# Six rotating PSUM banks outside the mixers, and a first feed forward that opens with four half-token results

## The chip, the cores and the metric

The kernel runs on one core of a Trainium2 chip. The time is that of the device, in microseconds (us), for one execution of the whole program. Before the change it is 1611.54 us, the median of 3 runs (1611.43 to 1612.52). The profile is one more execution, of 1611.52 us, whose span (first to last recorded instruction) is 1609.6 us.

## The reference

Two transformer blocks on 512 tokens of width 1024, in fp32. What matters here are the two feed forwards and the norms ahead of them:

```python
def first_block(x, c, ...):
    ...                                             # adaptive scales, sparse attention, retention, merge
    x = x + gate1 * jnp.dot(merged, w_out)
    h2 = _rmsnorm(x, norm2_w) * (1.0 + scale2) + shift2
    ffn = jnp.dot(jax.nn.silu(jnp.dot(h2, w_ffn_gate)) * jnp.dot(h2, w_ffn_up), w_ffn_down)
    x = x + gate2 * ffn
    return _rmsnorm(x, final_norm_w)

def second_block(x, ...):
    ...                                             # block-sparse attention, gated linear attention
    h = h + jnp.concatenate([o_nsa, o_gla], axis=-1) @ w_out
    u = causal_dwconv(rms_norm(h, ffn_norm) @ w_up, conv_w, conv_b)
    gate, up = jnp.split(u, 2, axis=-1)
    return h + (jax.nn.silu(gate) * up) @ w_down
```

The hidden width is 2816, that is 22 tiles of 128.

## The kernel before

Activations lie transposed: 128 features on the partitions, 512 tokens along a row. An fp32 product is made of three products (`mm3`, L298): activations and weights are each split into a high part and a rest, and high by high (L300), rest by high (L301) and high by rest (L302) are summed in one PSUM bank. "hH" and "hL" are the two parts of the activations, "wh" and "wl" those of a weight unit. A unit is one tile of 128 outputs by 8 tiles of 128 inputs, 512 KB. `load` (L280) fetches it into a staging tile "st" (3 buffers) by a DMA of SP's queue, ACT casts it to "wh" (L294) and DVE subtracts the rest "wl" (L295), each in two halves; "wh" and "wl" have 3 buffers each, so a fourth unit waits until the first is used up.

`projA` makes one tile of outputs for all 512 tokens: 24 products into one bank. `projM` makes several tiles at once, first for tokens 0 to 255 and then for tokens 256 to 511.

PSUM has eight banks. `ps` (L304) hands them out by tag: "mm" 3 banks for projections, "tr" 2 for transposes and small products, "pv" 1, and 2 for the attention scores ("at", or one tile of two banks; `scores` changes between the two forms). A projection takes an "mm" bank and must wait until the result that lay there three projections earlier has been read.

The end of block 1: `w_out` (L753) is done for tokens 0 to 255 and then for 256 to 511. After each half `norm2` (L629) does the norm: the sum of squares "acc" (L421, L422) goes through `tok_sum`, a product with a column of ones that puts the sums on the token's partition (L397); POOL takes the power -0.5 (L388, L389); `bcast` spreads the result over all partitions by products of ones and a diagonal "dg" (L409, L410); ACT copies that to "rbc" (L411); then for eight tiles DVE multiplies (L643), ACT or DVE scales and shifts (L648, L646), ACT casts "hH" (L380) and DVE or POOL makes "hL" (L381). These are the small products of the norm. While the second half of the tokens goes through this, `ffn1` (L997) has `projM` make the first half of three results: gate 0, up 0 and gate 1. From then on it uses `projA`: 22 pairs of gate and up, then 8 tiles of the down product.

The second feed forward `ffn2` (L1499) has no norm ahead of its products: they run on the raw sums, and each result is multiplied by "rbc" when DVE reads it from PSUM (L1517). So the banks of its first results come free only when the norm's broadcast is there.

The order of each engine's stream is set at build time, by a scheduler that takes instructions in the order in which the code issues them and moves them ahead where it finds a gap; `issue_after(x)` tells it to place an instruction only behind x. At run time each engine takes its stream strictly in order.

Of the kernel before, what the change touches and what calls it, by code (L numbers as in the profile page):

```python
# [8 lines left out]
F32 = mybir.dt.float32  # L9
F32R = mybir.dt.float32r  # L10
# [6 lines left out]
P = 128  # L17
# [149 lines left out]
class Builder:  # L167
    def __init__(self, nc, tc, ins, out, cdec, dbg=None):
        self.nc, self.tc, self.ins, self.out, self.cdec, self.dbg = nc, tc, ins, out, cdec, dbg or {}
        self.tasks, self.pend, self.ready = [], [], []  # L170
        self.order = self.plan()
        self.pools = {}
        self.every = 4
        self.deep = (4, 5)

# [98 lines left out]
    def ahead(self, n):  # L274

        while len(self.ready) < n and self.order:
            key = self.order.pop(0)
            self.ready.append((key, self.load(self.source(key))))

    def load(self, src, pool=None, eng=None):  # L280

        nc = self.nc
        a, b = src.shape[1], src.shape[2]
        n = a * b
        st = self.wp.tile([P, 1168], F32, name="st", tag="st", bufs=3)
        nc.sync.dma_start(st[:, 0:n], src.rearrange("p a b -> p (a b)"))
        if pool is None:
            hi = self.wp.tile([P, 1168], F32R, name="wh", tag="wh", bufs=3)
            lo = self.wp.tile([P, 1168], F32R, name="wl", tag="wl", bufs=3)
        else:  # L290
            hi, lo = [pool.tile([P, 1168], F32R, name=x) for x in ("wh0", "wl0")]
        cut = (a // 2) * b
        for x0, x1 in ((0, cut), (cut, n)):
            nc.scalar.copy(hi[:, x0:x1], st[:, x0:x1])  # L294
            (eng or nc.vector).tensor_tensor(lo[:, x0:x1], st[:, x0:x1], hi[:, x0:x1].bitcast(F32), op=ALU.subtract)  # L295
        return (hi[:, 0:n].rearrange("p (a b) -> p a b", b=b), lo[:, 0:n].rearrange("p (a b) -> p a b", b=b))
# [6 lines left out]

    def ps(self, tag):  # L304
        if tag == "at":
            return self.pa.tile([P, 512], F32, name="ps_at", tag="at", bufs=2) if self.apart else self.ps2()[0]
        return self.pp.tile([P, 512], F32, name="ps_" + tag, tag=tag, bufs={"mm": 3, "tr": 2, "pv": 1}[tag])
# [37 lines left out]

    def projM(self, keys, act):

        aH, aL = act
        U = [self.unit(x) for x in keys]
        ps = [self.ps("mm") for i in range(len(keys))]  # L350
        for hs in range(2):
            ts = slice(hs * 256, hs * 256 + 256)
            for n, ((H, L), p) in enumerate(zip(U, ps)):
                for k in range(8):
                    self.mm3(p[:, ts], H[:, k, :], L[:, k, :], aH[:, k, ts], aL[:, k, ts], k == 0, k == 7)
                if hs:
                    self.ahead(n + 1)
# [33 lines left out]
    def tok_sum(self, acc, name):  # L391
# [4 lines left out]
        for t in range(n):  # L396
            nc.tensor.matmul(ps[:, t:t + 1], acc[:, t * P:(t + 1) * P], self.ones[:, 0:1], start=True, stop=True)  # L397
        o = self.small.tile([P, NT], F32, name=name)
# [3 lines left out]
    def bcast(self, col, out):  # L402
# [4 lines left out]
        for t in range(n):  # L407
            dg = self.wk.tile([P, P], F32, name="dg", tag="dg", bufs=3)
            nc.vector.tensor_scalar(dg, self.c("ident"), col[:, t:t + 1], None, op0=ALU.mult)  # L409
            nc.tensor.matmul(ps[:, t * P:(t + 1) * P], self.ones, dg, start=True, stop=True)  # L410
        nc.scalar.copy(out, ps[:, 0:n * P])  # L411
# [122 lines left out]
    def build(self):  # L534
        nc, tc = self.nc, self.tc
        with tc.tile_pool(name="psum", bufs=1, space=PSUM) as self.pp, tc.tile_pool(name="dram", bufs=1, space=DRAM) as dp:
# [11 lines left out]
            self.ffn1()  # L548
            self.scores(True)
            self.block2_mix()  # L550
            self.close("scores")
            self.ffn2()
            self.close("x", "wk", "h", "w", "small", "cst")
# [75 lines left out]
    def norm2(self, acc, ts):  # L629

        nc = self.nc
        ss = self.tok_sum(acc, "ss2")
        rs = self.small.tile([P, NT], F32, name="rs2")
        n = acc.shape[1]
        self.rsq(rs[:, 0:n // P], ss[:, 0:n // P], 1.0 / D)
        rbc = self.wk.tile([P, S], F32, name="rbc", tag="rbc", bufs=2)
        self.bcast(rs[:, 0:n // P], rbc[:, 0:n])
        for j in range(8):
            if ts.start == 0:
# [12 lines left out]
    def block1_mix(self):  # L652
# [56 lines left out]
        with tc.manual_schedule(engines={mybir.EngineType.PE}):  # L709
# [4 lines left out]
            self.every = 4  # L714
        self.close("b1r", "b1a", "wa")
        self.dump("att", qaT)
        self.dump("y", y)
# [279 lines left out]
    def ffn1(self):  # L997
        nc, ins = self.nc, self.ins
        f1 = self.open("f1")
        first = self.projM([("wfg", 0), ("wfu", 0), ("wfg", 1)], self.act)  # L1000
        mods = self.add(self.mod_rest(40, 48), 0.25)
        mH = f1.tile([P, KF, S], F32R, name="fH")
        mL = f1.tile([P, KF, S], F32R, name="fL")
        for m in range(KF):
            pg = self.projA([("wfg", m)], self.act) if m > 1 else first[2 * m]
            s = self.wk.tile([P, S], F32, name="fs", tag="w2k", bufs=4)
            nc.scalar.activation(s, pg, AF.Silu)
            pu = self.projA([("wfu", m)], self.act) if m else first[1]
            nc.vector.tensor_tensor(s, pu, s, op=ALU.mult)
# [3 lines left out]
        nc.vector.tensor_tensor(self.fwan, self.v("final"), self.v("attn2"), op=ALU.mult)  # L1013
        acc1, acc2 = [f1.tile([P, S], F32, name=f"acc{i}") for i in range(2)]
        for m in range(8):
# [16 lines left out]
    def block2_mix(self):  # L1032
        nc, tc, ins = self.nc, self.tc, self.ins
        b2 = self.open("b2", "right")
        gmask = b2.tile([P, P], I32, name="gmask")
# [99 lines left out]
        self.finish()  # L1135
        self.close("gla", "wa", "bk")
        self.xT = self.open("x").tile([P, KD, S], F32, name="xT")
        po = self.open("o")
# [416 lines left out]
```

## Time and profile before

| what | value |
|---|---|
| time, median of 3 runs | 1611.54 us |
| the profiled execution | 1611.52 us |
| its span | 1609.6 us |
| PE busy | 1581.5 us, 98% |
| DVE busy | 952.1 us, 59% |
| ACT busy | 685.6 us, 43% |
| PE on the chain that ended last | 96% |

The PE (TensorE) is nearly always busy, so the table alone names no place to look at. The windows of 50 us do: in most of them PE is busy for all 50 us at a granted clock of 1.00, and in a few something is missing. A clock below 1.00 is a mean over the window of the two levels that TensorE has, 1.2 GHz and 2.4 GHz: 0.97 over 50 us means some 3 us at half clock.

### The profile page before, as it was taken

How to read it: one execution, taken by the hardware profiler on the slowest of the kernel's cores; microseconds unless marked ns; L12 is line 12 of the kernel's file. 1: busy time of each engine (PE TensorE's matmuls, PEld its weight loads, DVE VectorE, ACT ScalarE, POOL GpSimd, SP SyncE). 2: the span in 40 equal slices, each digit the busy share in tenths (PEclk: the TensorE clock that was granted, in tenths of full speed). 3: DMA queues.
4: the chain of work that ended last, by engine and by line, in shares of the span. 5: the costliest groups of instructions: out<-in, count | busy, mean ns of one | idle time of the engine just before them, and what ended most of it. 6: DMA issues, size and time to landing. Idle time of an engine off the chain costs nothing.

```text
span 1609.6 us, 23843 instructions
## 1 busy us (share of the span) xinstructions
PE 1581.5 (98%) x9093; PEld 1342.8 (83%) x9093; DVE 952.1 (59%) x2209; ACT 685.6 (43%) x1458; POOL 136.8 (8%) x290
## 2 busy tenths in 40 slices
PE   7999999999999999999999999999989999999999
PEld 5999888888888978888888899988768788888887
DVE  4468865477786764444333455676765777777221
ACT  4554765643223542232233334665643444444221
POOL 0130000121110110000000015100100000000000
PEclk9999999999999999999999999999999999999999
DMA  9223221236653533333333353121022222223331
GB/s 375 67 66 100 67 79 53 68 104 214 183 182 124 175 116 121 117 118 92 91 106 110 122 159 108 53 79 40 15 79 92 85 99 92 92 97 93 110 108 51
DMA packets 49440, 173.12 MB, mean 108 GB/s; under 512 B 6048, under 2 KB 6736, under 8 KB 48304
## 3 DMA queue, kind: packets, MB, share of 16 engines
q1 hardware_dynamic: 43376, 152.22, 29.5%
q0 software_dynamic: 5952, 19.40, 3.7%
q8 instruction: 71, 1.16, 0.3%
q14 instruction: 41, 0.34, 0.1%
HBM read 166.88 MB, written 4.19 MB: 106 GB/s over the span
## 4 chain that ended last, share of the span: by engine, by line
PE 96%; ACT 1%; DVE 1%; DMA 1%; issue 0%; POOL 0%; SPq 0%; POOLq 0%; ACTq 0%
PE ps_mm L300 28%; PE ps_mm L301 27%; PE ps_mm L302 27%; PE ps_tr L452 3%; PE ps_pv L506 2%; PE ps_at L1280 1%; PE ps_at L1229 1%; PE ps_at L891 1%; PE ps_at L833 1%; PE ps_at L966 0%; PE ps_at L1300 0%; DMA xs<-in_x_dram 0%; PE ps_pv L581 0%; PE ps_tr L410 0%; DMA xT<-xd 0%
## 5 line engine op out<-in xcount | busy, mean ns | idle before, releaser
L294 ACT CAST wh<-st 128x512 fp32r<-128x512 f32 (+3 forms) x508 | 283.7, 607 | 543.3 <-issue 265.9
L295 DVE TENSOR_TENSOR wl<-st,wh 128x512 fp32r<-128x512 f32 (+3 forms) x508 | 324.8, 670 | 172.1 <-ACT wh L294 170.2
L300 PE MATMUL ps_mm<-hH,wh 128*128 128x512 f32 (+1 forms) x1000 | 393.9, 394 | 4.4 <-DVE us L1517 2.2
L301 PE MATMUL ps_mm<-hL,wh 128*128 128x512 f32 (+1 forms) x1000 | 390.6, 391 | 0.3 <-DVE hL L381 0.3
L302 PE MATMUL ps_mm<-hH,wl 128*128 128x512 f32 (+1 forms) x1000 | 389.2, 390 | 0.0
L300 PEld LDWEIGHTS ps_mm<-hH,wh 128*128 128x128 f32 x1000 | 189.4, 189 | 45.1 <-DVE us L1517 2.4
L302 PEld LDWEIGHTS ps_mm<-hH,wl 128*128 128x128 f32 x1000 | 189.0, 189 | 41.0
L301 PEld LDWEIGHTS ps_mm<-hL,wh 128*128 128x128 f32 x1000 | 189.2, 189 | 38.6 <-DVE hL L381 0.5
L300 PE MATMUL ps_mm<-wh,hH 128*128 128x256 f32 (+2 forms) x672 | 192.8, 290 | 0.4 <-ACT hH L593 0.4
L301 PE MATMUL ps_mm<-wl,hH 128*128 128x256 f32 (+2 forms) x672 | 191.6, 287 | 0.0
L302 PE MATMUL ps_mm<-wh,hL 128*128 128x256 f32 (+2 forms) x672 | 189.1, 286 | 2.3 <-DVE hL L595 2.3
L300 PE MATMUL ps_mm<-fH,wh 128*128 128x512 f32 x352 | 138.8, 394 | 0.0
L301 PE MATMUL ps_mm<-fL,wh 128*128 128x512 f32 x352 | 138.7, 394 | 0.0
L302 PE MATMUL ps_mm<-fH,wl 128*128 128x512 f32 x352 | 138.5, 393 | 0.0
L300 PEld LDWEIGHTS ps_mm<-wh,hH 128*128 128x128 f32 x672 | 126.0, 188 | 5.2 <-issue 3.6
L302 PEld LDWEIGHTS ps_mm<-wh,hL 128*128 128x128 f32 x672 | 125.7, 189 | 3.4 <-DVE hL L595 2.8
L301 PEld LDWEIGHTS ps_mm<-wl,hH 128*128 128x128 f32 x672 | 126.4, 189 | 2.2 <-issue 1.4
L623 DVE SCALAR_TENSOR_TENSOR ma<-ms,silu_c,ma 128x128 f32<-128x128 f32 x224 | 77.3, 349 | 5.1
L300 PEld LDWEIGHTS ps_mm<-fH,wh 128*128 128x128 f32 x352 | 66.3, 188 | 15.4
L302 PEld LDWEIGHTS ps_mm<-fH,wl 128*128 128x128 f32 x352 | 66.1, 188 | 15.5
L301 PEld LDWEIGHTS ps_mm<-fL,wh 128*128 128x128 f32 x352 | 66.2, 188 | 15.1
L478 ACT ACTIVATE pm<-lt,mn 128x128 f32<-128x128 f32 (+3 forms) x96 | 53.8, 561 | 22.5 <-DVE mn L475 21.5
(376 smaller groups left out, 2195.2 us busy)
## 6 DMA issues: line engine op xcount, KB each, us to landing
st<-in_wup_dram SPq DMA_DIRECT2D x44, 512.0 KB, 3.3
ms<-in_wada_dram POOLq DMA_DIRECT2D x64, 256.0 KB, 3.4
st<-in_wo_dram SPq DMA_DIRECT2D x24, 512.0 KB, 3.5
st<-in_wfg_dram SPq DMA_DIRECT2D x22, 512.0 KB, 3.5
st<-in_wfu_dram SPq DMA_DIRECT2D x22, 512.0 KB, 3.5
wa<-in_wada_dram SPq DMA_DIRECT2D x8, 1024.0 KB, 11.6
st<-in_wret_dram SPq DMA_DIRECT2D x16, 512.0 KB, 3.6
st<-in_wfd_dram SPq DMA_DIRECT2D x16, 448.0 KB, 3.4
```

Source lines behind the costliest of these rows:

```text
L294: nc.scalar.copy(hi[:, x0:x1], st[:, x0:x1])
L295: (eng or nc.vector).tensor_tensor(lo[:, x0:x1], st[:, x0:x1], hi[:, x0:x1].bitcast(F32), op=ALU.subtract)
L300: mm(ps, lh, rh, start=start, stop=False)
L301: mm(ps, lh, rl, start=False, stop=False)
L302: mm(ps, ll, rh, start=False, stop=stop)
L452: return self.nc.tensor.transpose(out, src, self.c("ident", 0, n)[0:n])
L478: nc.scalar.activation(pm[:, 0:n], lt[:, 0:n], AF.Exp, bias=mn, scale=-1.0, accum_out=sm[:, a:a + 1])
L506: run(lambda: nc.tensor.matmul(pv()[a * 64:a * 64 + 64, j_, :], vtok(cc, 2 * j_ + a), PT_[a][:, cc * P:(cc + 1) * P], start=a not in start ...
L623: nc.vector.scalar_tensor_tensor(acc, w[:, k, :], s, acc, op0=ALU.mult, op1=ALU.add)
L833: nc.tensor.matmul(ps[:, 0:n], qS[:, h, :], ikS[:, i, 0:n], start=(i == 0), stop=(i == 1))
L891: run(lambda: nc.tensor.matmul(sc[:, 0:n], qaT[rows, h // 2, ts], kaT[rows, h // 2, 0:n], start=True, stop=True))
L1229: nc.tensor.matmul(ps[m][:, 0:64], w[:, i, m * P:(m + 1) * P], tb[:, ii, :, :].rearrange("p g n -> p (g n)"), start=(ii == 0), stop=(ii == ...
```

## The change

`ps` gets a counter "wide". While it is not None, every request for an "mm" bank is answered in turn with a bank of tag mm, at, mm, at, mm, pv: six banks that rotate. It is set to 0 at the end of block 1's mixers, taken away for those of block 2, and set again behind them. For this `scores(True)`, which brings the form with two single "at" banks, moves to the end of block 1's mixers, and the pool is closed only after `ffn2`.

`ffn1` opens with four half-token results instead of three: (up, 1) joins them. Its weights get a place of their own ("wh0", "wl0", in the pool f1), since the three usual buffers are taken. To make room, the two accumulators of `ffn1` move to the two "rbc" buffers of the pool wk. And two of the norm's small products get fixed places among the first half-token products: none from the 17th `mm3` on stands ahead of the sums (L397 before), none from the 27th on ahead of the broadcast (L410 before).

```diff
     def ahead(self, n):
-            self.ready.append((key, self.load(self.source(key))))
+            self.ready.append((key, self.load(self.source(key), pool=self.home.get(key))))
     def load(self, src, pool=None, eng=None):
-            hi, lo = [pool.tile([P, 1168], F32R, name=x) for x in ("wh0", "wl0")]
+            hi, lo = [pool.tile([P, n], F32R, name=x) for x in ("wh0", "wl0")]
     def ps(self, tag):
+        if tag == "mm" and self.wide is not None:
+            self.wide += 1
+            tag = ("mm", "at", "mm", "at", "mm", "pv")[self.wide % 6]
-    def projM(self, keys, act):
+    def projM(self, keys, act, between=()):
+        between = list(between)
+        count, behind = 0, None
...
                 for k in range(8):
-                    self.mm3(p[:, ts], H[:, k, :], L[:, k, :], aH[:, k, ts], aL[:, k, ts], k == 0, k == 7)
+                    if between and count == between[0][0]:
+                        behind = between.pop(0)[1]
+                    count += 1
+                    with self.tc.issue_after(behind) if behind is not None else contextlib.nullcontext():
+                        self.mm3(p[:, ts], H[:, k, :], L[:, k, :], aH[:, k, ts], aL[:, k, ts], k == 0, k == 7)
...
     def build(self):
             self.ffn1()
-            self.scores(True)
             self.block2_mix()
+            self.ffn2()
             self.close("scores")
-            self.ffn2()
     def norm2(self, acc, ts):
         ss = self.tok_sum(acc, "ss2")
+        sums = self.last
...
         self.bcast(rs[:, 0:n // P], rbc[:, 0:n])
+        self.marks = [sums, self.last]
     def block1_mix(self):
         self.close("b1r", "b1a", "wa")
+        self.scores(True)
+        self.wide = 0
     def ffn1(self):
-        first = self.projM([("wfg", 0), ("wfu", 0), ("wfg", 1)], self.act)
+        self.home["wfu", 1] = f1
+        first = self.projM([("wfg", 0), ("wfu", 0), ("wfg", 1), ("wfu", 1)], self.act, between=zip((16, 26), self.marks))
-            pu = self.projA([("wfu", m)], self.act) if m else first[1]
+            pu = self.projA([("wfu", m)], self.act) if m > 1 else first[2 * m + 1]
-        acc1, acc2 = [f1.tile([P, S], F32, name=f"acc{i}") for i in range(2)]
+        acc1, acc2 = [self.wk.tile([P, S], F32, name="acc", tag="rbc", bufs=2) for i in range(2)]
     def block2_mix(self):
+        self.wide = None
...
         self.close("gla", "wa", "bk")
+        self.wide = 0
```

What it moves stands in PE's stream at three places. The lines of the changed kernel are shifted: L302 to L304 are the three products, L409 the sums, L422 the broadcast.

First, PE where the first feed forward opens: the sums of squares of tokens 256 to 511 ("acc"). Before, they stand among the products of the third result (6495):

```order
L300 MATMUL ps_mm_6495<-hH_74,wh_6487 128x256
L301 MATMUL ps_mm_6495<-hL_75,wh_6487 128x256
L397 MATMUL ps_tr_6423<-ones_105,acc_6128 128x1 x2
L302 MATMUL ps_mm_6495<-hH_74,wl_6488 128x256
L300 MATMUL ps_mm_6495<-hH_74,wh_6487 128x256
L301 MATMUL ps_mm_6495<-hL_75,wh_6487 128x256
```

In the changed kernel:

```order
L303 MATMUL ps_mm_6506<-hL_75,wh_6399 128x256
L304 MATMUL ps_mm_6506<-hH_74,wl_6400 128x256
L409 MATMUL ps_tr_6427<-ones_105,acc_6132 128x1 x2
L302 MATMUL ps_at_6507<-hH_74,wh_6491 128x256
L303 MATMUL ps_at_6507<-hL_75,wh_6491 128x256
L304 MATMUL ps_at_6507<-hH_74,wl_6492 128x256
```

They moved from behind the 62nd of these products to behind the 48th, between the second result (6506) and the third (6507).

Second, PE at the same opening: the broadcast, and what follows it. Before:

```order
L301 MATMUL ps_mm_6495<-hL_75,wh_6487 128x256
L302 MATMUL ps_mm_6495<-hH_74,wl_6488 128x256
L410 MATMUL ps_tr_6432<-dg_6433,ones_105 128x128
L410 MATMUL ps_tr_6432<-dg_6436,ones_105 128x128
L300 MATMUL ps_mm_6493<-hH_74,wh_6358 128x256
L300 MATMUL ps_mm_6494<-hH_74,wh_6395 128x256
L300 MATMUL ps_mm_6495<-hH_74,wh_6487 128x256
```

In the changed kernel, where 6508 is the fourth result:

```order
L302 MATMUL ps_mm_6508<-hH_74,wh0_6499 128x256
L303 MATMUL ps_mm_6508<-hL_75,wh0_6499 128x256
L304 MATMUL ps_mm_6508<-hH_74,wl0_6500 128x256
L422 MATMUL ps_tr_6436<-dg_6437,ones_105 128x128
L422 MATMUL ps_tr_6436<-dg_6440,ones_105 128x128
L302 MATMUL ps_mm_6508<-hH_74,wh0_6499 128x256
L303 MATMUL ps_mm_6508<-hL_75,wh0_6499 128x256
```

Before, the products behind the broadcast are those of the second half of the tokens (of the results 6493 to 6495). Now 18 more first-half products of 6508 follow, and the second half begins behind them, in the same way: one product of each result, then tile by tile of the inputs over all four results, not result by result.

Third, PE where the second feed forward opens: the last of the four broadcast products there. Before, it stands ahead of the fourth result (12855):

```order
L300 MATMUL ps_mm_12816<-hH_74,wh_12745 128x512
L301 MATMUL ps_mm_12816<-hL_75,wh_12745 128x512
L302 MATMUL ps_mm_12816<-hH_74,wl_12746 128x512
L410 MATMUL ps_tr_12716<-dg_12726,ones_105 128x128
L300 MATMUL ps_mm_12855<-hH_74,wh_12784 128x512
L301 MATMUL ps_mm_12855<-hL_75,wh_12784 128x512
```

In the changed kernel, whose fourth result is 12878:

```order
L303 MATMUL ps_mm_12878<-hL_75,wh_12807 128x512
L304 MATMUL ps_mm_12878<-hH_74,wl_12808 128x512
L302 MATMUL ps_mm_12878<-hH_74,wh_12807 128x512
L303 MATMUL ps_mm_12878<-hL_75,wh_12807 128x512
L422 MATMUL ps_tr_12739<-dg_12749,ones_105 128x128
L304 MATMUL ps_mm_12878<-hH_74,wl_12808 128x512
L302 MATMUL ps_mm_12878<-hH_74,wh_12807 128x512
```

It stands 11 products later, inside the fourth result; its three fellows stay where they were, in the third.

On ACT the two halves of the cast of (up, 1) move from behind the last cast of "hH" to ahead of the copy of "rbc", and on DVE its two subtractions move from behind the norm's last "hL" to between the copy of the sums and the first "dg". At the start of block 2, DVE's three small instructions on the gains (L1163 to L1166) move from behind the sums' copies (L399) to ahead of them, and SP's loads of the gains and of the first weights of the compressed keys move ahead of one weight unit.

## Rows read from the trace of the kernel before

**Rows 1.** page part 1: busy time (share of the span), instructions

```profile
PE 1581.5 (98%) x9093; PEld 1342.8 (83%) x9093; DVE 952.1 (59%) x2209; ACT 685.6 (43%) x1458; POOL 136.8 (8%) x290
```

**Rows 2.** windows: us, PE, PEld, DVE, ACT, POOL busy, clock, DMA, GB/s

```profile
550.00:600.00 50.00, 46.98 (x286) 42.04 (x285) 31.90 (x68) 22.56 (x48) 9.02 (x13) 0.97 0.42 131
...
600.00:650.00 50.00, 50.00 (x218) 40.68 (x218) 23.05 (x47) 14.63 (x28) 2.15 (x4) 1.00 0.38 117
...
1100.00:1150.00 50.00, 49.00 (x426) 39.88 (x425) 35.55 (x117) 30.77 (x77) 6.68 (x8) 1.00 0.10 33
...
1150.00:1200.00 50.00, 44.10 (x350) 35.17 (x351) 34.36 (x88) 26.87 (x62) 4.71 (x8) 0.93 0.14 43
...
1250.00:1300.00 50.00, 47.81 (x201) 38.63 (x200) 36.64 (x56) 24.32 (x38) 0.00 (x0) 0.97 0.25 85
```

**Rows 3.** timeline of PE, first feed forward: start, us, what, [idle before]

```profile
553.99 0.28 PE L300 MATMUL ps_mm<-hH,wh 128*128 128x256 f32 x1
...
561.18 0.28 PE L301 MATMUL ps_mm<-hL,wh 128*128 128x256 f32 x1
...
561.29 0.50 PE L397 MATMUL ps_tr<-ones,acc 128*128 128x1 f32 x4
...
562.79 0.27 PE L302 MATMUL ps_mm<-hH,wl 128*128 128x256 f32 x1
...
563.60 0.68 PE L410 MATMUL ps_tr<-dg,ones 128*128 128x128 f32 x4 [0.53 <-DVE dg L409]
...
566.27 0.62 PE L300 MATMUL ps_mm<-hH,wh 128*128 128x256 f32 x3 [1.99 <-ACT hH L380]
...
567.18 0.39 PE L301 MATMUL ps_mm<-hL,wh 128*128 128x256 f32 x1 [0.29 <-DVE hL L381]
...
576.84 0.27 PE L302 MATMUL ps_mm<-hH,wl 128*128 128x256 f32 x1
...
577.31 0.50 PE L300 MATMUL ps_mm<-hH,wh 128*128 128x512 f32 x1 [0.20 <-ACT fs L1007]
```

**Rows 4.** timeline of ACT, DVE, POOL and SP, same place

```profile
574.21 1.14 ACT L294 CAST wh<-st 128x512 fp32r<-128x512 f32 x2 [2.79 <-PE ps_mm L301]
...
557.55 1.93 DVE L422 TENSOR_TENSOR acc<-acc,sq 128x256 f32<-128x256 f32 x4
...
563.16 0.48 DVE L409 TENSOR_SCALAR dg<-cst,rs 128x128 f32<-128x128 f32 x2 [1.18 <-POOL rs L389]
...
574.86 1.29 DVE L295 TENSOR_TENSOR wl<-st,wh 128x512 fp32r<-128x512 f32 x2 [3.01 <-ACT wh L294]
...
570.67 1.78 POOL L381 TENSOR_TENSOR hL<-nt,hH 128x256 fp32r<-128x256 f32 x2 [1.96 <-ACT hH L380]
...
552.58 0.33 SPq L286 DMA_DIRECT2D st<-in_wfu_dram  x1
```

**Rows 5.** DMA issues, 545 to 600 us: count, KB, us to landing

```profile
st<-in_wfu_dram SPq DMA_DIRECT2D x6, 512.0 KB, 3.7
```

**Rows 6.** timeline of PE, second feed forward

```profile
1251.64 0.38 PE L410 MATMUL ps_tr<-dg,ones 128*128 128x128 f32 x2
...
1254.21 0.65 PE L300 MATMUL ps_mm<-hH,wh 128*128 128x512 f32 x1 [2.19 <-DVE us L1517]
...
1257.96 0.40 PE L300 MATMUL ps_mm<-hH,wh 128*128 128x512 f32 x1
...
1261.48 0.40 PE L300 MATMUL ps_mm<-hH,wh 128*128 128x512 f32 x1
```

**Rows 7.** timeline of ACT and DVE, same place

```profile
1252.65 0.58 ACT L411 COPY rbc<-ps_tr 128x512 f32<-128x512 f32 x1
...
1253.47 1.28 DVE L1517 TENSOR_TENSOR us<-ps_mm,rbc 128x512 f32<-128x512 f32 x2
```

**Rows 8.** windows behind the two stalls: us, PE busy, clock, DMA, GB/s

```profile
568.24:571.77 3.53, 3.53 (x20) 0.52 0.00 0
...
1254.20:1258.00 3.80, 3.79 (x10) 0.55 0.44 138
```

More of the change, by code (lines that the diff above doesn't have):

```diff
@@ L170, in __init__ @@
         self.tasks, self.pend, self.ready = [], [], []
+        self.home = {}
         self.order = self.plan()
@@ L396, in tok_sum @@
         for t in range(n):
-            nc.tensor.matmul(ps[:, t:t + 1], acc[:, t * P:(t + 1) * P], self.ones[:, 0:1], start=True, stop=True)
+            self.last = nc.tensor.matmul(ps[:, t:t + 1], acc[:, t * P:(t + 1) * P], self.ones[:, 0:1], start=True, stop=True).ins
         o = self.small.tile([P, NT], F32, name=name)
@@ L409, in bcast @@
             nc.vector.tensor_scalar(dg, self.c("ident"), col[:, t:t + 1], None, op0=ALU.mult)
-            nc.tensor.matmul(ps[:, t * P:(t + 1) * P], self.ones, dg, start=True, stop=True)
+            self.last = nc.tensor.matmul(ps[:, t * P:(t + 1) * P], self.ones, dg, start=True, stop=True).ins
         nc.scalar.copy(out, ps[:, 0:n * P])
@@ L1033, in block2_mix @@
         nc, tc, ins = self.nc, self.tc, self.ins
+        self.wide = None
         b2 = self.open("b2", "right")
```

## The prediction

> **What bounds the kernel now.** I read the page first: PE is busy 98% of the span [rows 1], so nothing is won beside it, and all that can be won on it is some 28 us of idle time and what it does at half clock. The windows of 50 us say where that is [rows 2]. Most look like 600 to 650: busy 50.00 at clock 1.00. Two differ that this change touches: 550 to 600 (idle 3.0 us, clock 0.97) and 1250 to 1300 (idle 2.2 us, clock 0.97). The largest hole that a window shows in mid-program, 1150 to 1200 (idle 5.9 us, clock 0.93), lies in block 2's mixers, where PE's stream is the same before and after; I leave it as it is, 0.
>
> Then the timeline of PE at the first place [rows 3]. From 553.99 first-half products start every (561.18 - 553.99) / 61 = 0.118 us. The last starts at 562.79 and is done at about 562.9; then PE waits 0.53 us for "dg", does the broadcast at 563.60, waits 1.99 us for the first "hH" and 0.29 us for the first "hL". The other engines' timeline says why [rows 4]: this is the norm's chain, sums at 561.29, "dg" at 563.16, broadcast at 563.60, first "hH" at 566.27. The sums were placed late: the last addition to "acc" ended at 557.55 + 1.93 = 559.48, 1.8 us before PE took them. Behind the wait PE runs at half clock: 0.52 granted from 568.24 to 571.77 [rows 8]. The last sign is at 576.84 to 577.31: a product 0.47 us after the one ahead of it instead of 0.12, waiting for ACT's "fs", that is for the first of three banks to be read.
>
> The second place is simpler [rows 6, 7]. Three results are full at 1251.64. The fourth needs the first one's bank, which DVE reads at 1253.47, once "rbc" is there; ACT makes that at 1252.65, behind the last broadcast product at 1251.64. PE starts at 1254.21, after 2.19 us of idle, and then at a granted clock of 0.55 until 1258.0 [rows 8].
>
> **Place one, first feed forward.** *Added work.* (Up, 1) in two halves costs 24 more instructions, but two halves take 2 x 0.118 = 0.236 us, and one product of 512 columns (1261.48 - 1257.96) / 15 = 0.235 us [rows 3, 6]. So the split costs 24 x 0.001 us: nothing.
>
> *When the new order runs.* The sums now follow 48 products: 553.99 + 48 x 0.118 = 559.65, just behind the last addition at 559.48. They cost 0.3 us (561.18 to 562.79 holds 11 steps, 1.30 us, and took 1.61). Thirty products later, at 563.50, comes the broadcast's fixed place. Is "dg" ready? Sums to broadcast took 563.60 - 561.29 = 2.31 us, so 561.96 is the earliest; the two subtractions of (up, 1) now stand in this chain on DVE. Such a pair takes 1.29 us [rows 4], which gives 563.25 if none of it hides, still ahead of 563.50; if it hides beside POOL's power, 561.96. I take the second, but it decides nothing. Their input must be there: the load was issued at 552.58 and lands 3.7 us later [rows 4, 5]; ACT's last square precedes the last addition, which began at about 559.0, so a cast of 1.14 us behind it ends by 560.2. Before, that cast stood until 574.21 because it waited for a buffer that PE held [rows 4].
>
> From the broadcast on the chain is as before: first "hH" 2.67 us and first "hL" 3.58 us behind it, at 566.17 and 567.08. PE meanwhile has 18 more products (2.12 us) behind a broadcast of 0.4 to 0.7 us, so it arrives at about 566.2: the wait for "hH" is covered. It does four products of "hH" (0.47 us), waits some 0.4 us for "hL", and has 92 left: 567.08 + 92 x 0.118 = 577.9. The last parts are not late: POOL's last "hL" ended at 570.67 + 1.78 = 572.45 [rows 4], and the new order asks for it 55 products behind the first, at 573.6.
>
> *The sum.* Before, the same four results are done at 577.31 + 24 x 0.235 = 582.9. After: 577.9. **5.0 us less**: 24 products that now cover the wait (2.8), the half clock (3.53 x 0.48 = 1.7), the bank (0.35). That the clock stays up with 0.4 to 0.6 us of idle left is read from 1100 to 1150: 1.0 us of idle in all, in pieces, at clock 1.00 [rows 2].
>
> **Place two, second feed forward.** With six banks the fourth result needs none of the first three. It starts behind the third at 1251.64 and takes 24 x 0.235 = 5.6 us and at most 0.38 for the broadcast inside it [rows 6]: the fifth starts at about 1257.5, before at 1261.48. **4.0 us less** (2.19 idle, 3.8 x 0.45 = 1.7 of clock, the rest rounding). What is late next: the broadcast's last product now comes 11 products later, at 1254.2, and the first result is read 1.83 us behind it (as 1253.47 stands to 1251.64), at 1256.1. The seventh result is the first to need a bank of these, at 1257.5 + 2 x 5.6 = 1268.7: 12 us of slack. The weights: the fourth's and fifth's casts stand ahead of "rbc" on ACT, the sixth's too; the seventh's stands behind two activations, at about 1258, 10 us early.
>
> **The rest.** In the end of block 1's mixers and the steady feed forwards PE did not wait for a bank, so six change nothing there: 0, with 0.3 either way for the shuffled opening of the merge, where "aL" and "yL" pace PE. The accumulators share buffers with "rbc": the next "rbc" is written at block 2's start, long behind the sums that read them: 0. Block 2's opening has DVE's gains ahead of the sums' copies: 0 as long as their load is early.
>
> A rule that speaks against the change: in 600 to 650 three banks rotate all the time and the clock is 1.00 [rows 2]. The Trainium skill (TensorE: Matmul & The Clock Gate, A second HAM failure mode: psum-queue depth-cycling) says that cycling through PSUM banks can make PE pause between groups so often that its clock falls and rises again. By that rule the forecast would be rival 4 below; the trace at three banks does not bear it out.
>
> **Sum.** 5.0 + 4.0 = 9.0 us, against the profiled execution of 1611.52 us, which stands 0.02 us under the median: 1602.5 us.
>
> **Rivals.**
> 1. *The clock still falls at place one.* The remaining wait comes when PE's work is at its thinnest, and the norm's chain on DVE may slip behind the two subtractions. For it: the sums' margin is 0.17 us only. Against: PE now works through what was 3.4 us of near idleness. It gives back 1.7: 1604.2 us. Chance 0.14.
> 2. *Place two exchanges one wait for another.* "rbc" is 2.6 us later and DVE starts behind; if it can't keep weights coming, PE waits for "wl" instead of a bank and the 4.0 is lost: 1606.5 us. Against: DVE is busy 36.6 of 50 us there [rows 2], so it catches up. Chance 0.07. With rival 1 as well: 1608.2 us, 0.04.
> 3. *Slower, at block 2's opening.* The sums' copies on DVE now queue behind the gains' load; "rbc", "dg" and the reading of three banks hang on them. If the load lands late, PE stands still for the whole delay. It must come over 9 us late to turn the sum round; at 12 us, 1614.5 us. Against: the load moved ahead of a weight unit, not behind one. Chance 0.02.
> 4. *Bank cycling costs clock*, in this kernel as an episode like that at place two, 1.7 us, once per turn of six banks. There are some 160 results in the wide stretches, 27 turns: 46 us, 1648 us. The row at three banks is against it. Chance 0.01. The rule behind it is that of the Trainium skill named above.
>
> **How the numbers follow.** Forecast 0.72; its own range is 1601.3 (the remaining waits vanish too, and the merge gains a little) to 1603.8 (small new waits). The range for 8 in 10 takes in rivals 1 and 2: 1601.2 to 1606.6. A difference of 0.2% (3.2 us, up to 1608.3) is about what a measurement can tell from none. Faster: forecast, rivals 1 and 2, 0.93. Same: rivals 1 and 2 together, 0.04. Slower: 0.03.
>
> **What would show it.** Right: in PE's timeline at the first opening no gap over 0.6 us between the first of the 192 half-token products and the last, the clock at 1.00 throughout, the full-token products from some 577.9 on; at the second opening no wait of PE for "us", the clock at 1.00, and "us" read some 2.6 us later than before; the hole in block 2's mixers the same, earlier by 5 us. Wrong: PE waiting for "wl" behind the fourth result of either feed forward, a wait at the sums or the broadcast, or a clock below 1.00 in windows such as 600 to 650.

## The result, and the profile after

The changed kernel takes 1601.74 us (median of 6 runs, 1600.07 to 1603.39), beside 1612.09 us for the kernel before in the same comparison (6 runs, 1611.43 to 1614.99): ratio 0.9933, 95% interval 0.9920 to 0.9946. The forecast was 1602.5, range 1601.2 to 1606.6. Two later comparisons gave 0.9937 [0.9925, 0.9949] and 0.9943 [0.9931, 0.9956]. Of all runs below, one of three_with_places took 4390.28 us against 1603.68 to 1605.87 of its four others; its time there is the median of those four, and what held up the fifth is not known. The profiled execution is one of 1601.81 us, span 1599.9, against 1609.6: 9.7 us less.

Line numbers in the profile after are larger by 2 in `mm3` and by 12 to 18 further down. The windows of 50 us of the changed kernel (columns as in [rows 2]: length, busy time of PE, PEld, DVE, ACT and POOL, granted clock, DMA share, GB/s):

```profile
550.00:600.00 50.00, 49.82 (x332) 45.55 (x331) 33.58 (x71) 23.96 (x50) 9.17 (x12) 1.00 0.46 138
600.00:650.00 50.00, 50.00 (x219) 40.69 (x218) 22.86 (x45) 14.87 (x27) 2.68 (x5) 1.00 0.38 114
1150.00:1200.00 50.00, 45.45 (x328) 36.69 (x327) 33.35 (x80) 25.45 (x56) 2.64 (x6) 0.93 0.20 64
1250.00:1300.00 50.00, 50.00 (x218) 40.65 (x217) 41.51 (x65) 26.97 (x42) 0.00 (x0) 1.00 0.29 92
```

550 to 600 has 0.18 us of idle left where 3.0 stood, 1250 to 1300 none where 2.2 stood, and both are at clock 1.00 [rows 2]. 1150 to 1200 is still the hole it was. 600 to 650, now with six banks, is as full as with three.

PE's timeline at the opening of the first feed forward (start, duration, operation, idle time before and what ended it), the answer to [rows 3]:

```profile
554.16 0.28 PE L302 MATMUL ps_pv<-hH,wh 128*128 128x256 f32 x1
...
559.82 0.56 PE L409 MATMUL ps_tr<-ones,acc 128*128 128x1 f32 x4
...
563.87 0.61 PE L422 MATMUL ps_tr<-dg,ones 128*128 128x128 f32 x4
...
566.47 0.39 PE L302 MATMUL ps_pv<-hH,wh 128*128 128x256 f32 x1
...
567.39 0.39 PE L303 MATMUL ps_pv<-hL,wh 128*128 128x256 f32 x1 [0.18 <-DVE hL L393]
```

The sums (L409) and the broadcast (L422) stand at their places, neither waits, and of the waits for "dg", "hH" and "hL" (0.53, 1.99, 0.29) one of 0.18 us is left. All half-token products but those behind a wait or a small product follow at 0.12 us, and the first product of 512 columns starts here:

```profile
578.39 0.40 PE L302 MATMUL ps_at<-hH,wh 128*128 128x512 f32 x1
```

That is 24.23 us behind the opening's start. Before, the fourth of these results follows as 24 products of 512 columns from 577.31 on, and the product behind them starts at 582.94: 28.95 us. So 4.72 us are won in the opening itself.

DVE in the same stretch, after the last additions to "acc":

```profile
557.73 1.93 DVE L434 TENSOR_TENSOR acc<-acc,sq 128x256 f32<-128x256 f32 x4
560.42 0.16 DVE L411 COPY ss<-ps_tr 128x2 f32<-128x2 f32 x1 [0.76 <-PE ps_tr L409]
560.50 1.29 DVE L297 TENSOR_TENSOR wl<-st,wh 128x512 fp32r<-128x512 f32 x2
562.39 0.48 DVE L421 TENSOR_SCALAR dg<-cst,rs 128x128 f32<-128x128 f32 x2 [0.59 <-POOL rs L401]
```

and POOL there:

```profile
560.74 0.50 POOL L400 TENSOR_SCALAR rs<-ss 128x2 f32<-128x2 f32 x1 [7.41 <-DVE ss L411]
561.33 1.03 POOL L401 TENSOR_TENSOR rs<-rs,cst 128x2 f32<-128x2 f32 x1
```

The additions end at 559.66, 0.16 us before the sums are taken: that is all the margin there is. The two subtractions of (up, 1) stand between the sums' copy and "dg", beside POOL's power, as forecast.

PE at the opening of the second feed forward, the answer to [rows 6]:

```profile
1245.95 0.40 PE L302 MATMUL ps_mm<-hH,wh 128*128 128x512 f32 x1
...
1248.50 0.38 PE L422 MATMUL ps_tr<-dg,ones 128*128 128x128 f32 x2
...
1251.71 0.39 PE L302 MATMUL ps_at<-hH,wh 128*128 128x512 f32 x1
```

No row here has an idle time. The fourth result begins at 1245.95, straight behind the third, the broadcast's last products stand within it at 1248.50, and the fifth begins at 1251.71. DVE reads the first two results ahead of that ([rows 7] for before):

```profile
1249.54 0.69 DVE L1535 TENSOR_TENSOR us<-ps_at,rbc 128x512 f32<-128x512 f32 x1 [1.67 <-ACT rbc L423]
1250.14 0.68 DVE L1535 TENSOR_TENSOR us<-ps_mm,rbc 128x512 f32<-128x512 f32 x1
```

To see where the 9.7 us lie, each profile is cut at four instructions on PE: the opening's first half-token product, block 2's first transpose of "hl", the first product of block 2's output ("wo2"), and the end. All lengths in us, from PE's timelines; the runs below the second line are those of the experiments:

| profile | to the opening | opening to "hl" | "hl" to "wo2" | "wo2" to the end |
|---|---|---|---|---|
| before | 553.99 | 421.38 | 213.42 | 420.81 |
| after | 554.16 | 416.37 | 212.57 | 416.80 |
| after_again | 553.96 | 416.30 | 213.21 | 416.83 |
| after_third | 554.01 | 416.33 | 212.61 | 416.85 |
| no_second_banks | 552.55 | 416.32 | 214.60 | 420.83 |
| banks_only | 553.81 | 421.79 | 212.73 | 416.77 |
| four_no_places | 556.46 | 419.93 | 212.66 | 416.85 |
| three_with_places | 553.83 | 418.53 | 212.87 | 416.77 |
| places_early | 556.61 | 421.66 | 213.40 | 416.83 |
| fourth_bank_only | 553.85 | 416.29 | 213.24 | 416.82 |
| four_banks | 553.96 | 416.29 | 215.48 | 417.07 |
| xt_late | 556.73 | 416.30 | 207.47 | 416.80 |
| xt_late_again | 554.35 | 416.34 | 207.48 | 416.83 |

The second and the fourth column repeat within 0.1 us where the code in them is the same. Place one is worth 421.38 - 416.37 = 5.01 us, place two 420.81 - 416.80 = 4.01. What remains of the 9.7, 0.85 us less in the third column and 0.17 more in the first, is in the columns that vary from profile to profile.

### The profile page after: what moved, and what is told of

Its sections match the earlier page's. It is cut to its first block, busy times and chain, and to the rows that moved or that the text cites. A ratio compares the mean times of both kernels' runs of the same rounds, so it can differ in the third digit from the quotient of the medians.

```text
span 1599.9 us, 23805 instructions
## 1 busy us (share of the span) xinstructions
PE 1580.3 (99%) x9117; PEld 1343.0 (84%) x9117; DVE 950.3 (59%) x2209; ACT 686.2 (43%) x1458; POOL 137.5 (9%) x290
## 4 chain that ended last, share of the span: by engine, by line
PE 96%; ACT 1%; DVE 1%; DMA 1%; issue 0%; POOL 0%; SPq 0%; ACTq 0%; POOLq 0%
PE ps_mm L302 18%; PE ps_mm L303 18%; PE ps_mm L304 17%; PE ps_at L302 7%; PE ps_at L303 7%; PE ps_at L304 7%; PE ps_pv L302 3%; PE ps_pv L303 3%; PE ps_pv L304 3%; PE ps_tr L464 3%; PE ps_pv L518 2%; PE ps_at L1298 1%; PE ps_at L1247 1%; PE ps_at L906 1%; PE ps_at L848 1%; PE ps_at L981 0%
## 5 line engine op out<-in xcount | busy, mean ns | idle before, releaser
L302 PE MATMUL ps_mm<-hH,wh 128*128 128x512 f32 (+1 forms) x584 | 229.6, 393 | 0.0
L303 PE MATMUL ps_mm<-hL,wh 128*128 128x512 f32 (+1 forms) x584 | 227.2, 389 | 0.0
L304 PE MATMUL ps_mm<-hH,wl 128*128 128x512 f32 (+1 forms) x584 | 226.7, 388 | 0.0
L302 PE MATMUL ps_mm<-wh,hH 128*128 128x256 f32 (+2 forms) x672 | 193.3, 291 | 0.0
L304 PE MATMUL ps_mm<-wh,hL 128*128 128x256 f32 (+2 forms) x672 | 189.1, 286 | 0.8 <-DVE hL L606 0.8
L302 PEld LDWEIGHTS ps_mm<-wh,hH 128*128 128x128 f32 x672 | 126.4, 189 | 5.1 <-issue 3.6
L302 PEld LDWEIGHTS ps_mm<-hH,wh 128*128 128x128 f32 x584 | 110.1, 188 | 23.4 <-issue 1.1
L304 PEld LDWEIGHTS ps_mm<-hH,wl 128*128 128x128 f32 x584 | 109.7, 188 | 23.4
L303 PEld LDWEIGHTS ps_mm<-hL,wh 128*128 128x128 f32 x584 | 109.9, 188 | 21.7
L304 PEld LDWEIGHTS ps_mm<-wh,hL 128*128 128x128 f32 x672 | 125.7, 189 | 1.9 <-DVE hL L606 1.3
L302 PE MATMUL ps_at<-hH,wh 128*128 128x512 f32 (+1 forms) x280 | 109.2, 390 | 0.0
L303 PE MATMUL ps_at<-hL,wh 128*128 128x512 f32 (+1 forms) x280 | 108.3, 387 | 0.0
L304 PE MATMUL ps_at<-hH,wl 128*128 128x512 f32 (+1 forms) x280 | 108.2, 386 | 0.0
L302 PE MATMUL ps_mm<-fH,wh 128*128 128x512 f32 x176 | 69.3, 394 | 0.0
L304 PE MATMUL ps_mm<-fH,wl 128*128 128x512 f32 x176 | 69.2, 393 | 0.0
```

The source lines that it names most:

```text
L302: mm(ps, lh, rh, start=start, stop=False)
L303: mm(ps, lh, rl, start=False, stop=False)
L304: mm(ps, ll, rh, start=False, stop=stop)
```

## The experiments

The theory: the two places are separate; place one needs both the fourth result (cover) and the fixed places (an earlier chain), place two needs nothing but a free bank. Times stand against the changed kernel's 1601.74 (1601.75 and 1601.97 in the later comparisons; three_with_places, places_early, fourth_bank_only and the first xt_late ran beside the kernel before alone, which took 1612.11 there). Where a time and a column differ, the column decides, since it holds the place alone.

**after_again**, the changed kernel without an edit.

> The changed kernel once more, as the yardstick of its neighbours. Theory: 9.7 to 10.4 us less than the kernel before, ratio about 0.9935. In its first profile block 2's mixers gave 0.8 us more than forecast, because DVE waited 0.41 us for the residual's transfer (xT from xd) where the kernel before waited 1.4. If this belongs to the change, it shows again; if it is the transfer's luck, the wait differs from profile to profile and the gain there with it.

Measured: 1601.75 us (1600.08 to 1603.29), ratio 0.9937 [0.9925, 0.9949]. The third column is 213.21 now, not 212.57, and DVE's wait for the residual 0.60, not 0.41. So it is not the change's: over the eleven profiles that keep this code, before's among them, the column runs from 212.57 to 215.48. The longest has the longest single wait (1.93 us, in four_banks), but the wait alone doesn't order them: no_second_banks has 214.60 with 0.70 us in two parts, fourth_bank_only 213.24 with 1.93 in two parts. The rows of the kernel before show how such a wait acts; DVE, end of block 2's mixers:

```profile
1173.30 0.75 DVE L1141 SCALAR_TENSOR_TENSOR xT<-xT,vecs,rbc 128x512 f32<-128x512 f32 x1 [0.20 <-DMA xT<-xd]
1175.26 0.75 DVE L1141 SCALAR_TENSOR_TENSOR xT<-xT,vecs,rbc 128x512 f32<-128x512 f32 x1 [1.20 <-DMA xT<-xd]
1175.92 0.88 DVE L485 TENSOR_SCALAR pm<-pm,rs 128x512 f32<-128x512 f32 x2
```

and the changed kernel:

```profile
1167.08 0.75 DVE L1159 SCALAR_TENSOR_TENSOR xT<-xT,vecs,rbc 128x512 f32<-128x512 f32 x1 [0.41 <-DMA xT<-xd]
...
1169.76 0.88 DVE L497 TENSOR_SCALAR pm<-pm,rs 128x512 f32<-128x512 f32 x2
```

The scaling of the residual stands in DVE's stream ahead of "pm". While it waits for its transfer (1.20 us before, 0.41 after), "pm" waits behind it, and PE for "pm".

**no_second_banks**, three banks in the second feed forward:

```diff
         self.close("gla", "wa", "bk")
-        self.wide = 0
```

> Six banks switched on only from the end of block 1's mixers to block 2; the output product and the second feed forward of block 2 rotate through three again. Theory (the two places are separate, and the second is the bank wait alone): the wait for "us" of about 2.2 us is back with about 1.7 us of lost clock behind it, 4.0 us more than the changed kernel, some 1605.8. Rival (the place's gain came from the earlier work, not from the banks): within 1 us of the changed kernel.

Measured: 1606.38 us (1604.41 to 1608.49), ratio 0.9966 [0.9954, 0.9979], 4.6 us more; the fourth column is back to 420.83, the second stays at 416.32. PE's timeline at the fourth result:

```profile
1248.91 0.50 PE L302 MATMUL ps_mm<-hH,wh 128*128 128x512 f32 x1 [2.19 <-DVE us L1534]
```

and PE's windows around it (length, busy time, granted clock, DMA share, GB/s):

```profile
1250.00:1252.00 2.00, 2.00 (x7) 0.57 0.43 170
1252.00:1254.00 2.00, 2.00 (x6) 0.58 0.00 0
1254.00:1256.00 2.00, 2.00 (x10) 1.00 0.01 4
```

The same 2.19 us as in [rows 6], the same half clock behind them. Place two is the bank alone: 4.03 us in its column, where 4.0 were expected; the rest of the 4.6 is within what the other columns vary by.

**banks_only**, six banks, but three half-token results and no fixed places:

```diff
-        first = self.projM([..., ("wfg", 1), ("wfu", 1)], self.act, between=zip((16, 26), self.marks))
+        first = self.projM([..., ("wfg", 1)], self.act)
...
-            pu = self.projA([("wfu", m)], self.act) if m > 1 else first[2 * m + 1]
+            pu = self.projA([("wfu", m)], self.act) if m else first[1]
```

> Six banks as in the changed kernel, but the first feed forward opens with three half-token results and no fixed places. Theory: place two's 4.0 us stays, place one's is lost but for the bank (0.35 us): about 4.4 us more than the changed kernel, some 1606.1, with waits of PE for "hH" and "dg" of some 2 us and 0.5 us and a half clock behind them. Rival (the banks are what opened place one): no wait there, 1601.7.

Measured: 1607.81 us (1606.91 to 1610.18), ratio 0.9977 [0.9966, 0.9988], 6.1 us more, where 4.4 were expected. The fourth column keeps place two (416.77), the second loses all of place one (421.79). PE's timeline:

```profile
563.42 0.68 PE L422 MATMUL ps_tr<-dg,ones 128*128 128x128 f32 x4 [0.53 <-DVE dg L421]
566.09 0.58 PE L302 MATMUL ps_pv<-hH,wh 128*128 128x256 f32 x1 [1.99 <-ACT hH L392]
```

The waits for "dg" and "hH" of [rows 3] to the hundredth. The bank wait of 0.20 us is gone, yet the stretch is 0.4 us longer than before: the clock is at 0.50 in all of 566 to 572,

```profile
566.00:572.00 6.00, 5.91 (x26) 0.50 0.00 0
```

where it was 0.72 over the same six microseconds of the kernel before:

```profile
566.00:572.00 6.00, 5.44 (x30) 0.72 0.00 0
```

The expectation had the bank's 0.35 us kept and the half clock as before; the half clock is longer by more than that, and why is not known. Six banks alone win nothing at this place.

**four_no_places**, the fourth result, but no fixed places:

```diff
-        first = self.projM([..., ("wfu", 1)], self.act, between=zip((16, 26), self.marks))
+        first = self.projM([..., ("wfu", 1)], self.act)
```

> Four half-token results but no fixed places. The sums then stand 62 products behind the opening's start and the broadcast behind all 96, instead of 48 and 78. Theory (the places put the chain early enough, the results only cover it): broadcast at about 565.8, first "hH" 2.67 us later, nothing left for PE in between, so about 2.0 us of idle and 0.4 more for "hL", and 1.7 us of clock: 3.6 us more than the changed kernel, some 1605.3. Rival (the 24 more products alone cover the wait, 2.8 us of 5.0): 1603.9 or less. Second rival (the places do nothing): 1601.7.

Measured: 1605.84 us (1604.51 to 1607.74), ratio 0.9962 [0.9948, 0.9976], 4.1 us more; the second column 419.93, 3.6 more, which is what the theory gave. PE's timeline (this execution reached the opening 2.3 us later):

```profile
568.24 0.61 PE L422 MATMUL ps_tr<-dg,ones 128*128 128x128 f32 x4
570.84 0.39 PE L302 MATMUL ps_pv<-hH,wh 128*128 128x256 f32 x1 [1.99 <-ACT hH L392]
...
571.76 0.39 PE L303 MATMUL ps_pv<-hL,wh 128*128 128x256 f32 x1 [0.18 <-DVE hL L393]
```

Left to the scheduler, the broadcast stands behind all 96 products, and the whole wait for "hH" comes where no product is left. The added cover alone is worth 421.38 - 419.93 = 1.45 us of the 5.01, and the half clock behind the wait stays (a granted clock of 0.50 from 573 to 575).

**three_with_places**, the fixed places without the fourth result (the line on `pu` as in banks_only):

```diff
-        first = self.projM([..., ("wfg", 1), ("wfu", 1)], self.act, between=zip((16, 26), self.marks))
+        first = self.projM([..., ("wfg", 1)], self.act, between=zip((16, 22), self.marks))
```

> Three half-token results as before, but with fixed places: the sums behind 48 products, the broadcast behind 66 (18 products later, as early as its "dg" can be ready); six banks as in the changed kernel. Theory (places start the chain early, the fourth result's 24 products cover what is left of it): broadcast at 562.1 to 562.4, 1.5 us earlier than before; PE has 6 products left, waits some 1.4 us for "hH" and 0.2 to 0.4 for "hL"; four results are done 1.1 us later than in the changed kernel if the clock stays, 2.8 later if it falls: 1602.9 or 1604.6, the second taken. Rival (the places are enough by themselves): 1601.7, no wait over 0.5 us.

Measured: 1604.55 us (1603.68 to 1605.87), ratio 0.9956 [0.9943, 0.9969], 2.8 us more; the second column 418.53, 2.2 more than the changed kernel. PE's timeline:

```profile
562.07 0.60 PE L422 MATMUL ps_tr<-dg,ones 128*128 128x128 f32 x4
...
564.67 0.39 PE L302 MATMUL ps_pv<-hH,wh 128*128 128x256 f32 x1 [1.28 <-ACT hH L392]
...
565.59 0.39 PE L303 MATMUL ps_pv<-hL,wh 128*128 128x256 f32 x1 [0.29 <-DVE hL L393]
```

PE's window behind the waits (length, busy time, granted clock, DMA share, GB/s):

```profile
566.00:572.00 6.00, 5.94 (x49) 1.00 0.01 3
```

Broadcast and waits came as forecast; the clock stayed at 1.00, which the theory had not taken, and yet the stretch is longer than it gave for that case (1.1): four results take 26.05 us, 1.82 more than 24.23. So the time is the 1604.6 that was expected, but not for the reason given. The waits explain 1.28 + 0.29 - 0.18 = 1.39 of the 1.82; the rest is gaps of 0.1 to 0.2 us among the second half's products, most of them at products that read "hL". The fixed places alone are worth 421.38 - 418.53 = 2.85 us, more than the cover alone.

**places_early**, both places 24 products sooner:

```diff
-... between=zip((16, 26), self.marks))
+... between=zip((8, 18), self.marks))
```

> The changed kernel with both fixed places 24 products earlier: sums behind 24 products, broadcast behind 54. Theory (a place is worth something only where its input is there: the last addition ends at about 559.5, the sums would be asked at 557.0): PE stands 2.5 us in front of the sums, the chain starts no earlier than before, nothing is won behind it; 2.5 us more than the changed kernel if the clock stays, 4.2 if it falls: 1604.2 or 1605.9, the second taken. Rival (earlier is better, the cover hides it): 1601.7 or less.

Measured: 1605.23 us (1603.99 to 1610.36), ratio 0.9965 [0.9952, 0.9977]: 3.5 us more, between the two numbers. The profiled execution is the slowest of its runs; its second column is 421.66, 5.3 us more. PE's timeline there:

```profile
562.26 0.98 PE L409 MATMUL ps_tr<-ones,acc 128*128 128x1 f32 x4 [2.65 <-DVE acc L434]
...
569.37 0.61 PE L422 MATMUL ps_tr<-dg,ones 128*128 128x128 f32 x4
```

and PE's windows:

```profile
563.00:566.00 3.00, 3.00 (x15) 0.50 0.16 49
566.00:568.00 2.00, 2.00 (x12) 0.50 0.58 234
...
569.00:570.00 1.00, 1.00 (x10) 1.00 0.00 0
```

The chain begins no sooner than "acc" allows, PE stands 2.65 us in front of the sums and then runs at half clock until about 569. In this execution place one is lost whole, by the medians (3.5 of 5.0 us) two thirds of it: here a fixed place ahead of its input was about as bad as leaving the order to the scheduler.

**fourth_bank_only**, three rotating banks in the merge and the first feed forward, a bank of its own for the opening's fourth result:

```diff
         self.scores(True)
-        self.wide = 0
...
-        ps = [self.ps("mm") for i in range(len(keys))]
+        ps = [self.ps("at" if i == 3 else "mm") for i in range(len(keys))]
```

> As the changed kernel, but the merge and the first feed forward rotate through three banks as before; only the fourth result of its opening takes a bank of its own, and six rotate from block 2's output product on. Theory (in those stretches PE waits for no bank): 1601.7, within 0.5 us. Rival (six banks help in the steady stretch): over 0.5 us more. Second rival (cycling through six costs something): less than the changed kernel.

Measured: 1602.69 us (1601.73 to 1604.15), ratio 0.9944 [0.9931, 0.9957]. By the time alone, 0.9 us more, the first rival would hold. But the second and fourth columns of its profile (a run of 1601.97) are the changed kernel's (416.29, 416.82), so the 0.9 us does not come from the steady stretch; the other columns vary by more than that. Six banks do nothing there, for good or ill.

**four_banks**, four rotating banks in place of six:

```diff
-            tag = ("mm", "at", "mm", "at", "mm", "pv")[self.wide % 6]
+            tag = ("mm", "mm", "mm", "pv")[self.wide % 4]
```

> The changed kernel with four rotating banks in place of six, in the same stretches. Theory (place two needs just one bank more: the fifth result starts at 1251.7 in the changed kernel, and the first is read by DVE at 1249.5 to 1250.2): 1601.7 within 0.5 us, no wait of PE for "us". Rival (the spare banks matter, because the second and third result are read later): a wait for "us" at the fifth or sixth result, 1 to 3 us more.

Measured: 1602.47 us (1601.82 to 1604.57), 0.7 us more, ratio 0.9943 [0.9929, 0.9956]; no wait of PE for "us", the second column 416.29, the fourth 417.07 (0.2 to 0.3 more than with six). One bank more does nearly all of it. Its profile is of its slowest run; the third column is the long one, 215.48, with this row on DVE:

```profile
1171.17 1.41 DVE L1159 SCALAR_TENSOR_TENSOR xT<-xT,vecs,rbc 128x512 f32<-128x512 f32 x2 [1.93 <-DMA xT<-xd]
```

**xt_late**, a change of its own: the scaling of the residual behind the split of the gates.

```diff
-        (eng or self.nc.vector).tensor_tensor(lo, src, hi.bitcast(F32), op=ALU.subtract)
+        self.low = (eng or self.nc.vector).tensor_tensor(lo, src, hi.bitcast(F32), op=ALU.subtract).ins
...
             nc.sync.dma_start(self.xT[:, m, :], self.xd[m])
-            nc.vector.scalar_tensor_tensor(self.xT[:, m, :], ..., r1bc, ...)
...
             self.split(go[:, m, :], gH[:, m, :], gL[:, m, :])
+        with tc.issue_after(self.low): [nc.vector.scalar_tensor_tensor(self.xT[:, m, :], ..., r1bc, ...) for m in range(8)]
```

> The changed kernel with the scaling of the residual (8 instructions of 0.75 us on DVE, xT) moved from between block 2's last scores to behind the split of its gates. Theory (what is left at the end of the mixers, 4.6 to 6 us of idle and clock 0.93, is DVE's chain mn, pm, with these 8 and their transfer's wait standing in it; and the 0.8 us beyond the forecast in the first profile came from that wait): 6.0 us leave the chain, of which ACT's and PE's own steps give back some: 3.5 us less, about 1598.2 (1596.5 to 1599.5), and PE's wait for "pm" under 1 us. Rival (the chain is bound elsewhere): less than 1 us gained. Second rival (given back: DVE starts the output product 5.6 us behind and PE waits for "wl"): 1601 or more, with that wait in the trace.

Measured: 1597.46 us (1596.71 to 1599.16), ratio 0.9912 [0.9900, 0.9925]. The third column is 207.47, 5.1 to 5.7 us less than in the three profiles of the changed kernel. PE's waits (total, times, longest):

```profile
PE ps_at L1298 <- DVE mn L487: 0.6, 2, 0.3
PE ps_tr L464 <- DVE pm L497: 0.6, 1, 0.6
```

"pm" is down to 0.6 us from 2.0 to 4.1 in the profiles that kept the order, and the window 1150 to 1200 is at clock 1.00 (length, busy time, clock, DMA share, GB/s):

```profile
1150.00:1200.00 50.00, 47.11 (x370) 1.00 0.19 64
```

DVE shows the moved instructions, which end just ahead of the first addition that needs them:

```profile
1181.08 2.49 DVE L393 TENSOR_TENSOR gL<-go,gH 128x512 fp32r<-128x512 f32 x4
1183.49 5.38 DVE L1162 SCALAR_TENSOR_TENSOR xT<-xT,vecs,rbc 128x512 f32<-128x512 f32 x8
1188.93 0.69 DVE L1168 TENSOR_TENSOR xT<-ps_at,xT 128x512 f32<-128x512 f32 x1
```

PE waits for no "wl" (the fourth column is 416.80), so nothing is given back. The wait for the transfer was only 0.41 to 0.60 us in the three profiles of the changed kernel, so most of the 5.1 to 5.7 us can't come from the wait: the 5.4 us of scaling itself left the chain.

**after_third** and **xt_late_again**, side by side:

> The changed kernel once more, as the yardstick of the run behind it: 1601.7, with 416.3 us from the opening of the first feed forward to block 2's first transposes and 416.8 us from block 2's output product to the end, as in its first two profiles; the start-up and the end of block 2's mixers vary by about a microsecond.

> The version with the late scaling of the residual once more, beside the changed kernel on one chip. Theory: from block 2's first transposes to its output product 207.5 us as in the first look, against 212.6 to 213.2 in the changed kernel, and the time 4 to 5.5 us less. Rival (a part of its 4.3 us was the chip or the start-up): 2 us less or not even that.

Measured: 1601.97 us (1601.66 to 1605.47), ratio 0.9943 [0.9931, 0.9956], and 1596.74 us (1596.01 to 1598.34), ratio 0.9908 [0.9895, 0.9922]; third columns 212.61 and 207.48. The version beats both kernels: 5.2 us under the changed one in this comparison, 14.7 under the one before.

## Why the prediction was right

Both places came out at their size: 5.01 us for 5.0, 4.01 for 4.0, and each is undone by undoing its part alone. That place one met its figure to the hundredth is in part luck: 4.72 us of it were won in the opening, and 0.29 came from a stretch that the forecast put at 0. Point by point:

- *The split costs nothing.* The half-token products follow at 0.12 us, as before.
- *When the new order runs.* Sums at 559.82, as worked out (559.65, and an opening 0.17 us later); broadcast at 563.87 (563.50 + 0.17 = 563.67); no wait for "hH"; 0.18 us for "hL" (0.4 forecast). Most of the 0.20 us by which the broadcast is late is a count: from 561.18 to 562.79 of [rows 3] there are 10 steps, not 11 (the 62nd product to the 72nd and last), so the sums cost 0.43 us and not 0.3. Four results after 24.23 us, forecast 23.9.
- *What was won behind the opening.* From the end of the four results to "hl", before takes 392.43 us and the changed kernel 392.14, PE at clock 1.00 and without a wait in both. All ten profiles with the fourth half-token result take 392.13 to 392.15 there, the three without it (before, banks_only, three_with_places) 392.43 to 392.48. So these 0.29 us come with the fourth result, not with banks or places; by what means is not shown, and they are part of the 1.45 that four_no_places gives to the cover.
- *A term that was mis-sized without harm.* That "dg" is ready for a broadcast at 561.96 took POOL's power as it was. With the two subtractions beside it POOL's two instructions take 0.50 and 1.03 us; alone, in the kernel before, they took

```profile
562.15 0.20 POOL L388 TENSOR_SCALAR rs<-ss 128x2 f32<-128x2 f32 x1 [9.00 <-DVE ss L399]
562.43 0.70 POOL L389 TENSOR_TENSOR rs<-rs,cst 128x2 f32<-128x2 f32 x1
```

  So the subtractions don't hide beside the power for nothing: 0.63 us, and "dg" is begun at 562.39, 2.57 us behind the sums where it was 1.87 (563.16 - 561.29). The place was late enough to hide it. All ten profiles with the subtractions at this spot have 0.50 and 1.02 to 1.03 us, the three without them (before, banks_only, three_with_places) 0.20 and 0.70. The Trainium skill (GPSIMD Engine Reference, section 1, Specifications) says that POOL shares its interfaces to SBUF with VectorE and contends with DVE instructions that have two SBUF inputs; the subtraction is one, and the traces agree.
- *The sum of place one* was split into 2.8 of cover, 1.7 of clock and 0.35 of bank. The experiments divide it otherwise: places alone 2.85, cover alone 1.45, both 5.01, banks alone nothing (0.41 us longer in that profile). The parts need each other: the cover alone leaves a wait of 1.99 us for "hH" and the half clock behind it, the places alone one of 1.28 us, at clock 1.00; only both together leave none.
- *Place two.* No wait for "us", clock 1.00, the fifth result 68.61 us behind the first "wo2" product where it was 72.69. "us" is read 1.8 us later than before, counted the same way (66.44 against 64.68), not 2.6: the broadcast's last products do come 2.55 us later (65.40 against 62.85), but the first read follows 1.04 us behind them instead of 1.83, as ACT has no weight cast to finish ahead of "rbc" there (before, a cast of 1.14 us for two halves begins at 1251.61).
- *The rest at 0*: right; fourth_bank_only shows it for the merge and the steady stretch. Block 2's opening has no wait of PE for the gains.
- *Rival 1* (the clock falls) did not come; four_no_places and places_early show the two ways into it. *Rivals 2 and 3* did not come either. *Rival 4* is refuted: three, four and six banks give the same stretch in the first feed forward (416.29 to 416.37), four and six nearly the same in the second. The rule on cycling through PSUM banks in the Trainium skill (TensorE: Matmul & The Clock Gate, A second HAM failure mode: psum-queue depth-cycling), named in the prediction, speaks of pauses between groups; with six banks there are none here (600 to 650 above), so this kernel neither shows nor contradicts the fall of the clock that it describes.

The profile pair differed by 0.7 us more than the forecast: 0.85 in block 2's mixers and -0.17 in the start-up, both of the columns that vary whatever the kernel. The medians differ by 10.35 us, 1.35 more than the forecast; no run shows where the rest of that lies, and the changed kernel's own runs spread over 3.3 us. So the two places are confirmed by their columns, not by the time's nearness to 1602.5.

## What to carry to other kernels

When the only engine that matters waits for a chain on other engines, ask two things: does the chain start as early as its input allows, and is there independent work left for the wait. The first alone gave 2.9 us here, the second alone 1.5, both together 5.0. A fixed place must stand behind its input: 24 products too soon cost 3.5 us by the medians. And when instructions whose results are needed only later stand in an in-order stream, put them behind what the bound engine waits for: that was worth as much as the larger of the two places.

## What the runs showed of the hardware

- PE's clock after a wait: at the two places single waits of 1.99, 2.19 and 2.65 us were each followed by granted clocks of about 0.5 for some 3 to 7 us; 1.28 and 0.29 us, with three products between, left it at 1.00. The same two waits (0.53 and 1.99 us) were followed by 3.5 us of half clock in the kernel before and by some 6 in banks_only, so what a wait costs in clock is not one number.
- The start-up varies by itself: in three of the eleven profiles taken in the experiments the opening is reached at 556.5 to 556.7 instead of 552.6 to 554.4. PE's windows in one of them (xt_late):

```profile
24.00:32.00 8.00, 5.21 (x50) 0.87 1.03 420
32.00:40.00 8.00, 8.00 (x54) 0.71 0.94 385
```

  and in the same kernel's other profile (xt_late_again):

```profile
24.00:32.00 8.00, 7.00 (x57) 1.00 1.03 420
32.00:40.00 8.00, 8.00 (x74) 1.00 0.98 402
```

  PE is idle longer in the first (2.8 us against 1.0), while transfers run at 420 GB/s in both, and its clock falls. The idle time alone does not decide it: three_with_places is idle for 2.8 us in 24 to 32 too, and its clock is 1.00 there. All of this lies ahead of the change's first place. The spread of 3 us among the runs of one kernel is of this size; that it comes from there is not shown, since most runs have no profile.
